# Attention scores as three passes over split operands, the convolved x turned to tokens through DRAM, and branch sums and stream resting in DRAM

## The chip, the cores and the metric

The kernel is one program on 1 core of one Trainium2 chip. A core has a matrix engine (TensorE, PE in the profile), a vector engine (VectorE, DVE), an activation engine (ScalarE, ACT), a general engine (GpSimd, POOL) and a sequencer that issues DMAs (SyncE, SP). Each engine runs its own list of instructions in order, and semaphores make one wait for another. The metric is the device time of one execution in microseconds.

## The reference

Two blocks over 256 tokens of width 2048, all in float32. The first block runs a state-space branch and a gated linear attention branch side by side, merges them, and adds an MLP; the second block is two layers of attention with a gated output. What the change touches:

```python
xbc = silu(causal_depthwise_conv(xbc, conv_w, conv_b))       # 4096 columns of x, 1024 of B, 1024 of C
xs, Bm, Cm = split(xbc)
dt = softplus(dt_raw + dt_bias)
y = ssd_chunked(xs, dt, A, Bm, Cm) + D * xs                  # 64 heads of 64, 8 groups, chunks of 128 tokens
y = grouped_rms_norm(y * silu(z), norm_w, 8)
branch_ssd = y @ w_ssd_branch                                # 4096 -> 2048
merged = sigmoid(gate_ssd) * branch_ssd + sigmoid(gate_gla) * branch_gla
x = layer_norm(ALPHA * x + merged @ w_out)
x = layer_norm(ALPHA * x + squared_relu(x @ w_up) @ w_down)
# then two layers:
scores = q @ k.T * scale ; p = softmax(scores) ; o = p @ v   # three kinds of heads, 4 + 8 heads of 128
x = x + rms_norm((o * silu(gate)) @ w_out2) * norm_post
```

Every product is to be good to float32.

## The kernel before

**Products.** A weight matrix is read from DRAM as half units of 512 KB (`stage`, L128, tiles `ws`, five buffers), and each is split into a rounded high part `wh` (a cast on ACT, L136) and a rest `wl` (a subtraction on DVE, L137); both rings have five buffers. The activations are kept as such a pair too. One product of a 128-row tile is then three passes (`mm3`, L141 to L143: high by high, high by low, low by high) in the format float32r, each 128 x 128 stationary by up to 512 moving columns. The text calls one such pass of 512 columns a pass; a half unit has 12 of them.

**What sets the order.** `drive` walks through all half units in the order of the program. After each product its post-processing is started as a generator (`posts`), and after every second half unit (24 passes) each running generator is stepped once (`tick`). A `yield` in a post-processing therefore moves what follows it behind 24 more passes. The list so made is then ordered, engine by engine, by a scheduler that simulates time and moves an instruction back when it thinks its operands late; at run time each engine keeps that order.

**The state-space stage** (0 to about 650 us). For each of eight groups g there is a product for x and one for z of 96 passes each. `x_post` (L597) takes the x product: `conv_silu` turns it to channels through DRAM (`turn` and `regroup`: VectorE transposes 32 x 32 squares into `sq`, ACT issues four DMAs into the DRAM tile `turn`, SP loads it back as `tn`), convolves it, and leaves it in `xc` with channels on the partitions. Then TensorE turns `xc` back to tokens (L614, two blocks of four transposes), DVE scales that into `xdt`, `xw` and `y`, ACT makes the decay `E` from rows loaded by SP (L601, L624, L626), DVE multiplies it by `cbm` (L627), and TensorE makes `st`, two blocks of `y` and `yo`. `z_post` multiplies by the gate, norms, and turns the result through DRAM into `yT`, the operand of `ssd_branch` (two groups to an operand q; 48 passes for each of four columns n). The sums of the four q rest in four tiles `acc` of the pool `t4` (sixteen buffers of 4 KB a partition) from the first q until the merge.

**The attention layers** (about 2040 to 2857 us). `attend` (L1099) makes the scores of two heads at a time with plain float32 matmuls of 256 moving columns (L1112), the softmax on DVE and ACT, and the product by v. Its operands come from `to_T`, `to_T_t` and `up_T`, which copy the transposed q and k once. The stream `x` rests in four `t4` tiles through a layer and is updated at its end.

Of the kernel before, what the change touches and what calls it, by code (L numbers as in the profile page):

```python
# [17 lines left out]
P = 128  # L18
ST_BUFS, W_BUFS, T_BUFS, S_BUFS = 5, 5, 16, 6
D = 2048  # L20
T = 256
# [57 lines left out]
def tile_blocks(ctx, tc, a, out):  # L79
# [496 lines left out]
    def c_post(i, bh):  # L576
        def post(ps):
            CT = t4([P, 4, T], s="CT")
            yield from conv_silu(ps, 40 + 4 * i, CT)
            while not bh[0].done:  # L580
                yield
            for m in range(2):
                ps = aux([P, 4, P], "cb")
                for g in range(4):
                    nc.tensor.matmul(ps[:, g, :], BT[i][:, g, m * P:m * P + P], CT[:, g, m * P:m * P + P],
                                     start=True, stop=True)
                V.tensor_tensor(cbm[m][:, 4 * i:4 * i + 4, :], ps, U.unsqueeze(1).to_broadcast([P, 4, P]),
                                op=ALU.mult)
            S.copy(CT1[:, 4 * i:4 * i + 4, :], CT[:, :, P:T])
        return post  # L590
# [6 lines left out]
    def x_post(g, need):  # L597
        def post(ps):
            es = [t4([P, 8, P], s="E") for _ in range(2)]
            for m in range(2):  # L600
                nc.sync.dma_start(es[m], acs_rows[g, m].partition_broadcast(P))  # L601
            xc = t4([P, 4, T], s="xc")
            yield from conv_silu(ps, 4 * g, xc)
            for h in need:
                while not h[0].done:
                    yield
            hs = slice(8 * g, 8 * g + 8)
            y = ys[g] = t4([P, 2, 512], s="y")
            xdt = t4([P, 2, 512], s="xdt")
            xw = small([P, 512], "xw")  # L610
            for m in range(2):
                pt = aux([P, 512], "tr")
                for f in range(4):
                    nc.tensor.transpose(pt[:, f * P:f * P + P], xc[:, f, m * P:m * P + P], ident)  # L614
                V.tensor_tensor(heads8(xdt[:, m, :]), heads8(pt),
                                dt[:, m, hs].unsqueeze(2).to_broadcast([P, 8, 64]), op=ALU.mult)
                if m == 0:
                    V.tensor_tensor(heads8(xw), heads8(pt),
                                    dtw[:, hs].unsqueeze(2).to_broadcast([P, 8, 64]), op=ALU.mult)
                V.tensor_tensor(heads8(y[:, m, :]), heads8(pt),  # L620
                                Dbc[:, hs].unsqueeze(2).to_broadcast([P, 8, 64]), op=ALU.mult)
# [25 lines left out]
            V.tensor_tensor(y[:, 1, :], y[:, 1, :], yo, op=ALU.add)  # L647
        return post
# [26 lines left out]

    def ssd_branch(q, n, need):
        def post(ps):
            if q == 0:
                acc[n] = t4([P, 2, 512], s="acc")
            for m in range(2):  # L680
# [12 lines left out]
        return product(lambda: yop[q], [a["w_ssd"][8 * n + 2 * q + s] for s in range(2)], post, need)  # L693
# [216 lines left out]
    def merge(n):  # L910
# [12 lines left out]
        return product(lambda: og[0], [a["w_gla"][4 * n + s] for s in range(4)], post, need=ghs)  # L923
# [174 lines left out]
    def attend(o, pairs, vals, scale, bias=None):  # L1098
# [65 lines left out]

    def to_T(d, src, nft):

        for f in range(0, nft, 2):
            pt = aux([P, 2, T], "tr")
            transpose4(pt, src, f)
            S.copy(d[:, f:f + 2, :], pt)  # L1170

    def layer(l, x, hop, first, nxt):
# [10 lines left out]
        def pre():  # L1183
# [55 lines left out]
        def ckv_post(ps):  # L1239
# [9 lines left out]
            kpT = v["kpT"] = lay([P, 2, T], "kpT")  # L1249
            G.memset(kpT, 0.0)  # L1250
# [3 lines left out]
            for i in range(2):  # L1254
                S.copy(kpT[64 * i:64 * i + 64, i, :], pt[64 * i:64 * i + 64, :])
# [4 lines left out]
        def up_T(ws, op, s):  # L1260

            nk = 2 * len(ws)
            d = t4([P, 4, T], s=s)
            for f in (0, 2):
# [6 lines left out]
                S.copy(d[:, f:f + 2, :], pt)  # L1271
# [21 lines left out]
        def uqr_post(ps):  # L1293
            yield
            d = v["qpT"] = t4([P, 2, T], s="qpT")
# [31 lines left out]
        def akv_post(ps):  # L1327
# [6 lines left out]
            v["kaT"] = t4([P, 2, T], s="kaT")  # L1334
# [9 lines left out]
        def b_post_(ps):  # L1344
# [4 lines left out]
            def pairs(h, m):  # L1349
                ts = slice(m * P, m * P + P)  # L1350
                return [(v["qnT"][:, h, ts], v["knT"][:, h, :]), (v["qpT"][:, h // 2, ts], v["kpT"][:, h % 2, :])]
# [6 lines left out]
        def aq_post(i):  # L1358
            def post(ps):
# [3 lines left out]
                qaT = t4([P, 4, T], s="qaT")  # L1363
                yield from to_T_t(qaT, qa)
# [3 lines left out]
                yield from attend(o, lambda h, m: [(qaT[:, h, m * P:m * P + P], v["kaT"][:, i, :])],  # L1368
# [6 lines left out]
        def c_post_(i):  # L1375
            def post(ps):
# [4 lines left out]
                if i < 2:  # L1381
                    d = v["c", i] = t4([P, 4, T], s="cT")
                    yield from to_T_t(d, c)
# [6 lines left out]
                yield from attend(o, lambda h, m: [(v["c", 0][:, h, m * P:m * P + P], v["c", 1][:, h, :])],  # L1390
# [33 lines left out]
        def y_mid(n):  # L1424
            gb = []

            def pre():
# [4 lines left out]
                yg[n] = t4([P, 2, 512], s="yy")  # L1432

# [75 lines left out]

def _bias(rpb):  # L1510
# [13 lines left out]
def _layout(x):  # L1524
# [5 lines left out]
    cw = a["ssd_conv_w"][0]  # L1530
    o["vec"] = np.ascontiguousarray(np.concatenate(
        [_vec(cw[j]) for j in range(4)]
        + [_vec(a["ssd_conv_b"][0]), _vec(a["ssd_norm_w"][0]), _vec(a["gla_norm_w"][0]),
# [5 lines left out]
    o["w_in"] = np.concatenate([_blocks(w[:, c:c + NB]) for c in W_IN_COLS])  # L1539
# [39 lines left out]
```

## Time and profile before

| | |
|---|---|
| median of 3 runs | 2860.01 us (2857.66 to 2864.86) |
| profiled execution | 2858.03 us, its span 2856.3 us |
| PE busy | 2826.3 us, 99% |
| DVE, ACT busy | 1830.5 us (64%), 1423.6 us (50%) |
| moved by DMA | 617.82 MB, 216 GB/s |
| mean granted clock | 0.997 |

The matmuls are pipelined: the profile gives 0.39 us for one pass of 512 columns, though the next one starts 0.23 us after it. So the cost of a pass is read from the distance of two starts, and not from the length of one. A plain float32 matmul of 128 rows and 256 columns shows up as two records. An engine's idle time is only worth what it holds up: here that is TensorE.

### The profile page before, as it was taken

The page shows a single profiled execution, that of the slowest core. Times are in us where ns is not written, and L with a number is a line of the kernel's source. Part 1 is how long each engine was busy: PE and PEld are TensorE (multiplying, and loading weights), DVE is VectorE, ACT ScalarE, POOL GpSimd, SP SyncE. Part 2 cuts the span into 40 slices and gives each one's busy share as a digit, 9 for nine tenths or more (in the row PEclk, how much of TensorE's full clock was granted, in tenths as well). Part 3 has the DMA queues.
Part 4 walks back from the last instruction along what each step waited for, and adds up shares of the span by engine and source line. Part 5 has one row for each costly group of instructions (what it writes and reads, how often), then busy time and mean ns, then how long its engine had stood idle before and what let it go on. Part 6 is the DMA issues. An engine that isn't in the chain of part 4 may idle for free.

```text
span 2856.3 us, 35047 instructions
## 1 busy us (share of the span) xinstructions
PE 2826.3 (99%) x12928; PEld 2337.8 (82%) x12928; DVE 1830.5 (64%) x2393; ACT 1423.6 (50%) x2013; POOL 36.4 (1%) x49
## 2 busy tenths in 40 slices
PE   9999999999999999999999999999999999999998
PEld 7888888888887878887888888888788888798887
DVE  6877677775844846556665555566776556676564
ACT  5565655554444544445344443344565544655543
POOL 0000000000000000000000000000000000000000
PEclk9999999999999999999999999999999999999999
DMA  8666666666665666674666666667467776567774
GB/s 287 221 226 219 221 221 221 220 221 215 186 198 169 213 200 213 218 269 161 229 227 222 221 212 221 207 222 252 147 217 236 234 238 219 164 214 242 249 234 142
DMA packets 209839, 617.82 MB, mean 216 GB/s; under 512 B 23665, under 2 KB 65009, under 8 KB 209666
## 3 DMA queue, kind: packets, MB, share of 16 engines
q1 hardware_dynamic: 163874, 573.62, 61.2%
q10 hardware_dynamic: 45792, 41.96, 4.7%
q8 instruction: 101, 1.65, 0.2%
q14 instruction: 72, 0.59, 0.1%
HBM read 571.90 MB, written 43.58 MB: 215 GB/s over the span
## 4 chain that ended last, share of the span: by engine, by line
PE 83%; DMA 7%; DVE 4%; ACT 3%; issue 1%; ACTq 1%; SPq 0%; DVEq 0%; POOLq 0%
PE mm L141 26%; PE mm L143 26%; PE mm L142 26%; DMA turn<-sq 3%; DMA tn<-turn 2%; DVE wl L137 2%; DMA ws<-in_w_in 1%; ACT wh L136 1%; PE sc L1112 1%; PE y L637 1%; ACTq L338 1%; DMA E<-acs_rows 1%; PE po L1144 1%; DVE sq L328 0%; PE up L143 0%
## 5 line engine op out<-in xcount | busy, mean ns | idle before, releaser
L137 DVE TENSOR_TENSOR wl<-ws,wh 128x1024 fp32r<-128x1024 f32 (+2 forms) x974 | 1167.9, 1210 | 750.0 <-ACT wh L136 739.8
L136 ACT CAST wh<-ws 128x1024 fp32r<-128x1024 f32 (+2 forms) x974 | 1005.3, 1044 | 979.4 <-PE mm L143 798.0
L141 PE MATMUL mm<-wh,xh 128*128 128x512 f32 x1280 | 503.9, 395 | 0.6 <-ACT wh L136 0.6
L142 PE MATMUL mm<-wl,xh 128*128 128x512 f32 x1280 | 499.8, 391 | 1.1 <-DVE wl L137 1.1
L143 PE MATMUL mm<-wh,xl 128*128 128x512 f32 x1280 | 499.2, 390 | 0.0
L141 PE MATMUL mm<-wh,lnh 128*128 128x512 f32 (+1 forms) x896 | 345.2, 389 | 5.9 <-ACT lnh L304 5.9
L142 PE MATMUL mm<-wl,lnh 128*128 128x512 f32 (+1 forms) x896 | 347.2, 387 | 0.0
L143 PE MATMUL mm<-wh,lnl 128*128 128x512 f32 (+1 forms) x896 | 346.5, 387 | 0.0
L141 PEld LDWEIGHTS mm<-wh,xh 128*128 128x128 f32 x1280 | 240.8, 188 | 55.5 <-issue 3.6
L142 PEld LDWEIGHTS mm<-wl,xh 128*128 128x128 f32 x1280 | 241.0, 188 | 53.6 <-DVE wl L137 2.5
L143 PEld LDWEIGHTS mm<-wh,xl 128*128 128x128 f32 x1280 | 240.9, 188 | 50.4
L141 PEld LDWEIGHTS mm<-wh,lnh 128*128 128x128 f32 x896 | 168.4, 188 | 40.2 <-ACT lnh L304 6.9
L143 PE MATMUL mm<-wh,hT 128*128 128x512 f32 x512 | 199.2, 389 | 0.0
L141 PE MATMUL mm<-wh,hT 128*128 128x512 f32 x512 | 199.2, 389 | 0.0
L142 PE MATMUL mm<-wl,hT 128*128 128x512 f32 x512 | 199.2, 389 | 0.0
L143 PEld LDWEIGHTS mm<-wh,lnl 128*128 128x128 f32 x896 | 168.5, 188 | 34.3 <-DVE lnl L305 0.9
L142 PEld LDWEIGHTS mm<-wl,lnh 128*128 128x128 f32 x896 | 168.5, 188 | 33.4 <-DVE wl L137 0.2
L141 PE MATMUL mm<-wh,hh 128*128 128x512 f32 (+1 forms) x384 | 148.2, 387 | 3.5 <-ACT hh L304 3.5
L142 PE MATMUL mm<-wl,hh 128*128 128x512 f32 (+1 forms) x384 | 148.0, 385 | 0.6 <-DVE wl L137 0.6
L143 PE MATMUL mm<-wh,hl 128*128 128x512 f32 (+1 forms) x384 | 147.1, 384 | 0.0
L141 PEld LDWEIGHTS mm<-wh,hT 128*128 128x128 f32 x512 | 96.1, 188 | 20.0
L143 PEld LDWEIGHTS mm<-wh,hT 128*128 128x128 f32 x512 | 96.1, 188 | 19.9
(366 smaller groups left out, 3403.3 us busy)
## 6 DMA issues: line engine op xcount, KB each, us to landing
ws<-in_w_in SPq DMA_DIRECT2D x494, 512.0 KB
ws<-in_w_up SPq DMA_DIRECT2D x128, 512.0 KB
ws<-in_w_down SPq DMA_DIRECT2D x128, 512.0 KB
ws<-in_w_out SPq DMA_DIRECT2D x96, 512.0 KB
turn<-sq ACTq DMA_DIRECT2D x316, 128.0 KB
tn<-turn SPq DMA_DIRECT2D x79, 512.0 KB
ws<-in_w_ssd SPq DMA_DIRECT2D x64, 512.0 KB
ws<-in_w_gla SPq DMA_DIRECT2D x32, 512.0 KB
```

Of the source, the lines that this page charges most:

```text
L136: S.copy(hi[:, c], st[:, c])
L137: V.tensor_tensor(lo[:, c], st[:, c], f32(hi[:, c]), op=ALU.subtract)
L141: nc.tensor.matmul(ps, l[0], r[0], start=first, stop=False)
L142: nc.tensor.matmul(ps, l[0], r[1], start=False, stop=False)
L143: nc.tensor.matmul(ps, l[1], r[0], start=False, stop=last)
L338: S.dma_start(dv[q], sv[32 * q:32 * q + 32, :].rearrange("j (b r) -> j b r", b=4))
L637: nc.tensor.matmul(py[:, h * 64:h * 64 + 64], es[m][:, h, :], xdt[:, m, h * 64:h * 64 + 64], start=True, stop=True)
L1112: nc.tensor.matmul(ps[:, m, :], l, rr, start=n == 0, stop=n == len(lr) - 1)
L1144: nc.tensor.matmul(po[:, m, :], pT[:, 2 * i + k, m * P:m * P + P], vals(h, k), start=k == 0, stop=k == 1)
```

## The change

- **Scores.** Every operand of a score is kept as a pair of float32r tiles, a rounded copy (ACT) and the rest (a new subtraction on DVE), and each score is made by `mm3`, three passes of 256 columns, in place of one float32 matmul. `kpT` is cleared by a memset of a scratch tile and two casts.
- **Convolved x.** `x_post` no longer uses TensorE: DVE transposes squares of `xc`, `regroup` takes them through DRAM (four DMAs on ACT, one load on SP), and the three scalings read the loaded tile. The columns of x are permuted in the weights for that (`_quarters`). The loads of `E` are issued behind this round trip, where before they were issued at the start of `x_post`.
- **Branch sums.** After each `ssd_branch` the sum goes to DRAM (a DMA on ACT) and is loaded back before the next one and before the merge.
- **Stream.** At the start of each attention layer `x` goes to DRAM, and each quarter is loaded back for its output product.
- **Steps.** `c_post` and both uses of `to_T_t` in the attention get one more `yield`.

```diff
-    def to_T_t(d, src):
+    def to_T_t(d, src, parts=None):
...
-            S.copy(d[:, :, m * P:m * P + P].rearrange("p c (q i) -> p c q i", q=4), by_token(got[0], m))
+            h, l = ((x[:, :, m * P:m * P + P].rearrange("p c (q i) -> p c q i", q=4) for x in parts) if parts else
+                    (d[:, :, m * P:m * P + P].rearrange("p c (q i) -> p c q i", q=4), None))
+            S.copy(h, by_token(got[0], m))
+            if parts:
+                V.tensor_tensor(l, by_token(got[0], m), f32(h), op=ALU.subtract)
...
             yield from conv_silu(ps, 40 + 4 * i, CT)
+            yield
             while not bh[0].done:
...
     def x_post(g, need):
         def post(ps):
-            es = [t4([P, 8, P], s="E") for _ in range(2)]
-            for m in range(2):
-                nc.sync.dma_start(es[m], acs_rows[g, m].partition_broadcast(P))
             xc = t4([P, 4, T], s="xc")
             yield from conv_silu(ps, 4 * g, xc)
             for h in need:
                 while not h[0].done:
                     yield
             hs = slice(8 * g, 8 * g + 8)
+
+            sq = t4([P, 4, 2, 4, 32], s="sq")
+            for m in range(2):
+                V.transpose(sq[:, :, m].rearrange("p a f j -> p f a j"),
+                            xc[:, :, m * P:m * P + P].rearrange("p f (a i) -> p f a i", a=4))
+            got = []
+            yield from regroup(sq, got)
+            xt = got[0].rearrange("p b m f j -> p b m (f j)")
+            es = [t4([P, 8, P], s="E") for _ in range(2)]
+            for m in range(2):
+                nc.sync.dma_start(es[m], acs_rows[g, m].partition_broadcast(P))
...
-            for m in range(2):
-                pt = aux([P, 512], "tr")
-                for f in range(4):
-                    nc.tensor.transpose(pt[:, f * P:f * P + P], xc[:, f, m * P:m * P + P], ident)
-                V.tensor_tensor(heads8(xdt[:, m, :]), heads8(pt),
-                                dt[:, m, hs].unsqueeze(2).to_broadcast([P, 8, 64]), op=ALU.mult)
+            for m in range(2):
+                by_head(xdt[:, m, :], m, dt[:, m, hs])
                 if m == 0:
...
+                    by_head(xw, m, dtw[:, hs])
+                by_head(y[:, m, :], m, Dbc[:, hs])
...
+    acc_rest = [dram.tile([P, 1024], F32, tag=f"acc{n}", name=f"acc{n}") for n in range(4)]
+
+    def acc_load(n):
+        acc[n] = t4([P, 2, 512], s="acc")
+        nc.sync.dma_start(acc[n].rearrange("p m n -> p (m n)"), acc_rest[n])
...
+        def pre():
+            if q:
+                acc_load(n)
+
...
+            S.dma_start(acc_rest[n], acc[n].rearrange("p m n -> p (m n)"))
...
                     for n, (l, rr) in enumerate(lr):
-                        nc.tensor.matmul(ps[:, m, :], l, rr, start=n == 0, stop=n == len(lr) - 1)
+                        mm3(ps[:, m, :], l, rr, n == 0, n == len(lr) - 1)
...
-            S.copy(d[:, f:f + 2, :], pt)
+            S.copy(d[0][:, f:f + 2, :], pt)
+            V.tensor_tensor(d[1][:, f:f + 2, :], pt, f32(d[0][:, f:f + 2, :]), op=ALU.subtract)
+
+
+    x_rest = [dram.tile([P, 1024], F32, tag=f"xs{n}", name=f"xs{n}") for n in range(4)]
...
                     sumsq(x[n][:, m, :], parts[m][:, n:n + 1])
+                nc.sync.dma_start(x_rest[n], x[n].rearrange("p m n -> p (m n)"))
...
-                qaT = t4([P, 4, T], s="qaT")
-                yield from to_T_t(qaT, qa)
+                qaT = two(4, "qaT")
+                yield from to_T_t(None, qa, qaT)
+                yield
...
                 yg[n] = t4([P, 2, 512], s="yy")
+                x[n] = t4([P, 2, 512], s="xs")
+                nc.sync.dma_start(x[n].rearrange("p m n -> p (m n)"), x_rest[n])
```

Three places show where the order of the instructions moved. The first is TensorE in the state-space stage, at group 1: `y` and `yo` are its last products (`E` and `st` its operands), `mm_2107` before and `mm_2070` in the change are the z product of group 2, behind which the first `ssd_branch` product follows. Before:

```order
L142 MATMUL mm_1870<-wl_1941,xh_81 128x512
L143 MATMUL mm_1870<-wh_1940,xl_82 128x512
L637 MATMUL y_2061<-xdt_1902,E_1649 128x64 x8
L643 MATMUL yo_2071<-st_2013,CT_43_109 128x512
L141 MATMUL mm_2107<-wh_1975,xh_81 128x512
L142 MATMUL mm_2107<-wl_1976,xh_81 128x512
```

In the change:

```order
L141 MATMUL mm_2070<-wh_2084,xh_81 128x512
L142 MATMUL mm_2070<-wl_2085,xh_81 128x512
L143 MATMUL mm_2070<-wh_2084,xl_82 128x512
L651 MATMUL y_2106<-xdt_1992,E_1987 128x64 x8
L651 MATMUL y_2154<-xdt_1992,E_1988 128x64 x8
L657 MATMUL yo_2164<-st_2104,CT_43_109 128x512
L141 MATMUL mm_2070<-wh_2084,xh_81 128x512
```

Before, `yo` stands ahead of the first of the 96 passes of that z product; in the change 63 of them are past. The first passes that read the `yT` half of group 1 are the 25th of the `ssd_branch` product in both, so 120 passes lie between before, and 57 in the change.

The second is SP, where the two loads of `E` for group 1 stand (`ws` are weight half units, `tn` a tile loaded back from DRAM). Before:

```order
L128 DMA ws_1426<-in_w_in 128x1024
L128 DMA ws_1446<-in_w_in 128x1024
L601 DMA E_1648<-acs_rows 128x1024
L601 DMA E_1649<-acs_rows 128x1024
L128 DMA ws_1485<-in_w_in 128x1024
```

In the change:

```order
L128 DMA ws_1955<-in_w_in 128x1024
L341 DMA tn_1949<-turn_1908 128x1024
L128 DMA ws_1973<-in_w_in 128x1024
L620 DMA E_1987<-acs_rows 128x1024
L620 DMA E_1988<-acs_rows 128x1024
L128 DMA ws_2011<-in_w_in 128x1024
```

The loads moved behind `tn_1949`, the load that ends the new round trip of `xc`, and with it behind the wait of that load for its DRAM writes.

The third is ACT in the first attention layer, at the second block of four `a` heads: `turn` is the DRAM write of the turned q, `qaT` (`qaTh`) the copy that the scores wait for. Before:

```order
L338 DMA turn_17335<-sq_17332 32x4x256 x4
L136 CAST wh_17515<-ws_17362 128x1024
L1147 ACTIVATE ao_17157<-po_17381,rec_17168 128x128 x2
L1147 ACTIVATE ao_17157<-po_17388,rec_17179 128x128 x2
L136 CAST wh_17535<-ws_17401 128x1024
L1138 COPY pT_17433<-tn_17376 128x4x128 x2
L136 CAST wh_17593<-ws_17419 128x1024
L374 COPY qaT_17331<-tn_17395 128x4x128 x2
```

In the change:

```order
L338 DMA turn_17497<-sq_17494 32x4x256 x4
L136 CAST wh_17699<-ws_17526 128x1024
L136 CAST wh_17717<-ws_17567 128x1024
L1164 COPY pT_17542<-tn_17492 128x4x128 x2
L136 CAST wh_17776<-ws_17585 128x1024
L136 CAST wh_17794<-ws_17623 128x1024
L1173 ACTIVATE ao_17302<-po_17545,rec_17317 128x128 x2
L376 CAST qaTh_17446<-tn_17502 128x4x128 x2
```

Four casts of weights stand between the write and the copy where there were three. On TensorE the scores moved further: the cast ahead of the write is released by a pass that is 51 passes ahead of these scores before, and 84 in the change.

## Rows read from the trace of the kernel before

**Rows 1.** The page, parts 1 and 4: busy time; chain by line.

```profile
PE 2826.3 (99%) x12928; PEld 2337.8 (82%) x12928; DVE 1830.5 (64%) x2393; ACT 1423.6 (50%) x2013; POOL 36.4 (1%) x49
...
PE mm L141 26%; PE mm L143 26%; PE mm L142 26%; DMA turn<-sq 3%; DMA tn<-turn 2%; DVE wl L137 2%; DMA ws<-in_w_in 1%; ACT wh L136 1%; PE sc L1112 1%; PE y L637 1%; ACTq L338 1%; DMA E<-acs_rows 1%; PE po L1144 1%; DVE sq L328 0%; PE up L143
```

**Rows 2.** Two stretches: each engine's busy us (count), clock, DMA.

```profile
140.00:660.00 520.00, 518.32 (x2414) 427.71 (x2413) 378.75 (x529) 303.06 (x474) 5.58 (x8) 1.00 0.68 222
1400.00:1600.00 200.00, 200.00 (x884) 165.65 (x883) 116.37 (x117) 82.16 (x86) 0.00 (x0) 1.00 0.68 223
```

**Rows 3.** Timeline of PE: passes of a plain product.

```profile
1000.08 0.39 PE L141 MATMUL mm<-wh,xh 128*128 128x512 f32 x1
...
1008.70 0.39 PE L143 MATMUL mm<-wh,xl 128*128 128x512 f32 x1
```

**Rows 4.** Timeline of PE: one block of four transposes at line 614.

```profile
158.79 0.39 PE L143 MATMUL mm<-wh,xl 128*128 128x512 f32 x1
159.03 0.60 PE L614 MATMUL tr<-cst,xc 128*128 128x128 f32 x4
...
159.93 0.40 PE L143 MATMUL mm<-wh,xl 128*128 128x512 f32 x1
```

**Rows 5.** Instructions of lines 1112 and 614, whole span.

```profile
0.00:2857.00 2857.00, 38.75 (x160) 30.96 (x160) 1.00 0.66 216
0.00:2857.00 2857.00, 9.75 (x64) 8.03 (x64) 1.00 0.66 216
```

**Rows 6.** Timeline of PE: first and last score of one block.

```profile
2132.67 0.59 PE L1112 MATMUL sc<-knT,qnT 128*128 128x256 f32 x2
...
2139.15 0.59 PE L1112 MATMUL sc<-kpT,qpT 128*128 128x256 f32 x2
```

**Rows 7.** Timeline of PE: split passes of 256 columns.

```profile
2125.80 0.28 PE L143 MATMUL up<-kvh,wl 128*128 128x256 f32 x1
...
2126.52 0.29 PE L143 MATMUL up<-kvh,wl 128*128 128x256 f32 x1
```

**Rows 8.** Waits of PE, by what ended them.

```profile
PE sc L1112 <- ACT qaT L374: 4.4, 2, 3.3
...
PE cb L585 <- DVE CT L557: 1.2, 2, 0.8
```

**Rows 9.** Timeline of PE: scores behind a wait of 3.26 us.

```profile
2218.77 3.66 PE L1112 MATMUL sc<-kaT,qaT 128*128 128x256 f32 x8 [3.26 <-ACT qaT L374]
2221.86 0.82 PE L141 MATMUL mm<-wh,lnh 128*128 128x512 f32 x1
```

**Rows 10.** Granted clock (behind POOL's column) after that wait.

```profile
2220.00:2224.00 4.00, 4.00 (x14) 3.13 (x13) 2.58 (x5) 2.86 (x11) 0.00 (x0) 0.71 0.41 122
```

**Rows 11.** Timeline: group 1 from yo to its yT's reader.

```profile
231.31 1.13 PE L643 MATMUL yo<-st,CT 128*128 128x512 f32 x2 [0.57 <-ACT st L633]
243.88 2.04 ACTq L338 DMA_DIRECT2D turn<-sq  x4
251.37 0.33 SPq L341 DMA_DIRECT2D tn<-turn  x1
257.74 1.13 DVE L366 SCALAR_TENSOR_TENSOR yT<-tn,vec,yT 128x128 fp32r<-128x128 f32 x4
259.52 0.39 PE L141 MATMUL mm<-wh,yT 128*128 128x512 f32 x1
```

**Rows 12.** Timeline of ACT: eight instructions on one tile E.

```profile
224.10 2.46 ACT L624 ACTIVATE E<-E,acs 128x128 f32<-128x128 f32 x8 [4.84 <-DMA E<-acs_rows]
```

**Rows 13.** Chain in order of time: two transfers, issue to landing.

```profile
185.62 4.32 DMA turn<-sq
...
216.24 7.83 DMA E<-acs_rows
```

**Rows 14.** Groups by line: DVE on E.

```profile
L627 DVE TENSOR_TENSOR E<-E,cbm 128x1024 f32<-128x1024 f32 x16 | 19.5, 1218 | 5.8 <-ACT E L626 5.8
```

**Rows 15.** The page, part 2: all DMA traffic.

```profile
DMA packets 209839, 617.82 MB, mean 216 GB/s; under 512 B 23665, under 2 KB 65009, under 8 KB 209666
```

More of the change, by code (lines that the diff above doesn't have):

```diff
@@ L692, in post @@
             yield
-        return product(lambda: yop[q], [a["w_ssd"][8 * n + 2 * q + s] for s in range(2)], post, need)
+        return product(lambda: yop[q], [a["w_ssd"][8 * n + 2 * q + s] for s in range(2)], post, need, pre=pre)
     def gate_tanh(col, row, n):
@@ L922, in post @@
                 yield from to_op(mg, 4, *mop[0], 4 * n, mul=0.5)
-        return product(lambda: og[0], [a["w_gla"][4 * n + s] for s in range(4)], post, need=ghs)
+        return product(lambda: og[0], [a["w_gla"][4 * n + s] for s in range(4)], post, need=ghs,
+                       pre=lambda: acc_load(n))
     gate_tanh(GG0, 1, 0)
@@ L1163, in attend, with two, part @@
         yield
+    def two(nft, s):
+        if nft == 2:
+            d = t4([P, 2, 2, T], F32R, s=s)
+            return d[:, 0], d[:, 1]
+        return t4([P, nft, T], F32R, s=s + "h"), t4([P, nft, T], F32R, s=s + "l")
+    def part(ap, *i):
+        return tuple(x[i] for x in ap)
     def to_T(d, src, nft):
@@ L1248, in ckv_post @@
             yield from to_op(ckv, 2, *v["ckv"], 0, scale=vec[:, V_KVN + 2 * l:V_KVN + 2 * l + 2])
-            kpT = v["kpT"] = lay([P, 2, T], "kpT")
-            G.memset(kpT, 0.0)
+            kpT = v["kpT"] = tuple(lpool[0].tile([P, 2, T], F32R, tag=f"kpT{i}", name=nm("kpT")) for i in range(2))
+            zero = small([P, 512], "zero")
+            G.memset(zero, 0.0)
+            for i in range(2):
+                V.tensor_copy(kpT[i], zero.rearrange("p (i t) -> p i t", i=2))
             pt = aux([P, T], "tr")
@@ L1254, in ckv_post @@
             for i in range(2):
-                S.copy(kpT[64 * i:64 * i + 64, i, :], pt[64 * i:64 * i + 64, :])
+                hs = slice(64 * i, 64 * i + 64)
+                S.copy(kpT[0][hs, i, :], pt[hs, :])
+                V.tensor_tensor(kpT[1][hs, i, :], pt[hs, :], f32(kpT[0][hs, i, :]), op=ALU.subtract)
         cqj = product(hopf, w2(0), cq_post, need=first, pair=(0,))
@@ L1262, in up_T @@
             nk = 2 * len(ws)
-            d = t4([P, 4, T], s=s)
+            d = two(4, s)
             for f in (0, 2):
@@ L1270, in up_T @@
                             (op[0][:, k, :], op[1][:, k, :]), k == 0, k == nk - 1)
-                S.copy(d[:, f:f + 2, :], pt)
+                S.copy(d[0][:, f:f + 2, :], pt)
+                V.tensor_tensor(d[1][:, f:f + 2, :], pt, f32(d[0][:, f:f + 2, :]), op=ALU.subtract)
             return d
@@ L1294, in uqr_post @@
             yield
-            d = v["qpT"] = t4([P, 2, T], s="qpT")
+            d = v["qpT"] = two(2, "qpT")
             to_T(d, v["qp"], 2)
@@ L1333, in akv_post @@
             yield
-            v["kaT"] = t4([P, 2, T], s="kaT")
+            v["kaT"] = two(2, "kaT")
             to_T(v["kaT"], ka, 2)
@@ L1350, in pairs @@
                 ts = slice(m * P, m * P + P)
-                return [(v["qnT"][:, h, ts], v["knT"][:, h, :]), (v["qpT"][:, h // 2, ts], v["kpT"][:, h % 2, :])]
+                al = slice(None)
+                return [(part(v["qnT"], al, h, ts), part(v["knT"], al, h)),
+                        (part(v["qpT"], al, h // 2, ts), part(v["kpT"], al, h % 2))]
             yield from attend(o, pairs, lambda h, k: v["vb"][:, k, h * P:h * P + P], 192.0 ** -0.5)
@@ L1367, in post @@
                 o = v["o", i] = t4([P, 2, 512], s="ao")
-                yield from attend(o, lambda h, m: [(qaT[:, h, m * P:m * P + P], v["kaT"][:, i, :])],
+                yield from attend(o, lambda h, m: [(part(qaT, slice(None), h, slice(m * P, m * P + P)), part(v["kaT"], slice(None), i))],
                                   lambda h, k: v["va"][:, k, i * P:i * P + P], 128.0 ** -0.5)
@@ L1381, in post @@
                 if i < 2:
-                    d = v["c", i] = t4([P, 4, T], s="cT")
-                    yield from to_T_t(d, c)
+                    d = v["c", i] = two(4, "cT")
+                    yield from to_T_t(None, c, d)
                     yield
@@ L1389, in post @@
                 o = v["o", 3] = t4([P, 2, 512], s="ao")
-                yield from attend(o, lambda h, m: [(v["c", 0][:, h, m * P:m * P + P], v["c", 1][:, h, :])],
+                yield from attend(o, lambda h, m: [(part(v["c", 0], slice(None), h, slice(m * P, m * P + P)), part(v["c", 1], slice(None), h))],
                                   lambda h, k: v["c", 2][:, k, h * P:h * P + P], 128.0 ** -0.5, a["c_bias"][l])
@@ L1507, in _vec, with _quarters @@
     return np.asarray(v).reshape(-1, P).T
+def _quarters(w):
+    return w.reshape(w.shape[0], -1, 4, 4, 32).transpose(0, 1, 3, 2, 4).reshape(w.shape)
 def _bias(rpb):
@@ L1529, in _layout @@
     o["consts"] = _consts()
-    cw = a["ssd_conv_w"][0]
+    cw, cb = (np.concatenate([_quarters(v[:, :4096]), v[:, 4096:]], axis=1)
+              for v in (a["ssd_conv_w"][0], a["ssd_conv_b"]))
     o["vec"] = np.ascontiguousarray(np.concatenate(
         [_vec(cw[j]) for j in range(4)]
-        + [_vec(a["ssd_conv_b"][0]), _vec(a["ssd_norm_w"][0]), _vec(a["gla_norm_w"][0]),
+        + [_vec(cb[0]), _vec(a["ssd_norm_w"][0]), _vec(a["gla_norm_w"][0]),
            _vec(a["ln1_g"][0]), _vec(a["ln1_b"][0]),
@@ L1538, in _layout @@
     w = a["w_in"][0]
-    o["w_in"] = np.concatenate([_blocks(w[:, c:c + NB]) for c in W_IN_COLS])
+    o["w_in"] = np.concatenate([_blocks(_quarters(w[:, c:c + NB]) if XBC0 <= c < XBC0 + 4096 else w[:, c:c + NB])
+                                for c in W_IN_COLS])
     o["w_dtlr"] = _blocks(np.concatenate([w[:, LR0:LR0 + 16], w[:, DT0:DT0 + 64]], axis=1), 16, 80)[0]
```

9 lines of the change are left out of this document (5 added, 4 removed).

## The prediction

> **What bounds the kernel now.** The page's busy times come first, and the chain by line beside them: TensorE is busy 99% of the span, and three quarters of the chain that ended last are the three passes of a product [rows 1]. Then the table of stretches, for the state-space stage and, as a comparison, for a stretch of plain products at the full clock: in the first TensorE is busy 518.3 of 520 us, while DVE works 379 and ACT 303 [rows 2]. So DVE and ACT have 27% and 42% of that stage free, and work added there costs only what it makes late. The unit of the sum is a pass: 38 passes in 8.62 us, 0.2268 us each [rows 3]. An edit thus counts in two ways: work taken off TensorE, and an operand that comes later than the passes between its producer and its reader give it time for.
>
> The sum is made on the profiled execution (2858.03 us, its span 2856.3). The median of the runs is 2.0 us higher, and the forecast is stated against that median. About 0.3%, or 8.6 us, is what a measurement of this kernel can tell from no change.
>
> **Transposes of x, removed.** A block of four stands between starts 158.79 and 159.93; of these 1.14 us three passes are 0.68, so four transposes cost 0.46 [rows 4]. There are 64 of them [rows 5], 16 blocks: -7.4 us.
>
> **Scores.** 160 records are 80 matmuls [rows 5]. From the first to the last of a block of 16 are 15 steps in 6.48 us, 0.432 each [rows 6], 34.6 us in all. A float32r pass with the same 256 columns costs 0.120 (six steps in 0.72) [rows 7]; 240 of them are 28.8 us. So -5.8 us.
>
> [...]
>
> **Waits that go.** The scores of the a heads wait 4.4 us for `qaT`, in two places, 3.3 in the longer [rows 8]. [...] Together 3.26 + 1.4 + 1.1 in the other layer, some 6 us. By the order of TensorE the cast ahead of the q write is released 84 passes before these scores instead of 51: 33 passes, 7.5 us, more than the 3.3 it was late, though one more cast and a subtraction stand in the path. So -6 us, bounds 0 (the wait stays) and -6. What comes late next would be the low half, one subtraction behind the copy. The wait of `cb` for `CT`, 1.2 us [rows 8], goes with the extra step of 24 passes: -1.2.
>
> The gains are 7.4 + 5.8 + 6.0 + 1.2 = 20.4 us.
>
> **A wait that comes: the first `ssd_branch`.** Its passes read the `yT` of group 1. Before, `yo` of group 1 starts at 231.31, and the first reader of the `yT` half that ends last starts at 259.52, when that half has been done since 258.87 (257.74 + 1.13): 0.65 us to spare [rows 11]. What lies between is gate, norm, squares, four writes on ACT at 243.88, the load on SP at 251.37 and the four operations of DVE, 27.6 us in all. In the change `y` and `yo` stand 63 passes later, because the operand comes by a round trip first, and the reader has not moved: 57 passes for 120. 63 x 0.2268 = 14.3 us less, minus the 0.65 to spare: 13.6 us of idle TensorE. If the second `y` also waits for `E`, up to 2 us more. If TensorE stands still the casts run ahead, and ACT and DVE serve the chain sooner: 12.6 us of it lie between `yo` and the write, with casts and squares among them, of which 1 to 8 may go. I take 13, bounds 7 and 17. Queued behind the waiting pass are all weights of that product; nobody else needs TensorE's result meanwhile, and what was missed is not made up since every later pass follows in order. After the idle time the clock falls as in rows 10; an idle 3.26 us cost 1.4 there, a longer one I put at 2, bounds 1.4 and 5. So +15. The later q have a whole product more between (168 passes, 38 us, for a chain of 27.6) and do not wait.
>
> The round trip's own length is in the trace: the write took 4.32 us from issue to landing [rows 13], and from the write's issue at 243.88 to the load's at 251.37 are 7.5 us, to the DVE operations behind it some 4 more [rows 11], so about 11.5. [...]
>
> **`E` behind the round trip.** Its load now starts after the trip: turn 4 to 5 us, `tn` 4 to 5, `E` 7.8 [rows 13], two times 2.46 on ACT [rows 12], two exponentials at 1.05 on ACT, and 1.2 on DVE [rows 14]: about 25 us from the turn to the first `y`. By the order `y` stands about that far behind in the groups 0 and 2 to 7, with 1 to 2 us to spare. Such a spare is met in most groups and missed by little in some: I take one miss of 3 us, the spread between the transfers counted above, as the nearer value, with bounds 0 and 24 (3 us in each of 8 groups).
>
> **What is hidden.** DVE gets 16 transposes of squares, about 11 us, in a stage where it has 141 us free; low parts in the attention, some 20 us, where TensorE's share is as high. ACT gets 32 issues for the turns, four of them in 2.04 us [rows 11], and 16 for the sums; SP 40 loads and stores, whose waits stand ahead of weight loads in its list. DMA gets 64 transfers of 512 KB, 33.6 MB, 5% of 617.82 [rows 15]; the stage moves 222 GB/s and its queues are busy 0.68 [rows 2]. Cover is the ring of weights: five `ws` and five `wh` tiles of 12 passes, 27 us of products. As long as a wait on SP or a burst is shorter than that it costs nothing: 0, and if the cover is gone, a bound of +10.
>
> **Sum.** -20.4 + 15 + 3 = -2.4 us: 2855.6 by the profiled execution, about 2857.5 by the median.
>
> **Rivals.** *No long wait* (faster): the chain behind `yo` shrinks because TensorE's stop sets free what it shares ACT and DVE with, and `E` comes in time. -20.4 + 7 + 1.4 = -12, so 2848. For it: ACT's casts stand inside the chain. Against it: the two DMA waits in it, 11.5 us, don't shrink. *`E` late in each group* (slower): the path to `E` is as long as the passes give it time for; with 3 us in each of 8 groups in place of 3 in all, the sum is -20.4 + 15 + 24 = +18.6, so 2878.5. The place is the first `y` of each group; it decides once `E` is later than 2 us beyond my count. For it: before, `E` already took 7.83 us to land and ACT waited 4.84 for it [rows 12, 13]. Against it: E's path is counted with 4 to 5 us for each way, which is what loaded queues show. *The stream of weights suffers* (slower): SP's waits for its round trips hold up weight loads, or 5% more traffic in bursts empties the ring; the bound of +10 on top of the sum gives +7.6, 2867.5, and with the waits' clock some 2871. Against it: 27 us of cover. *The score wait stays* (no change): the extra step is eaten by the extra casts, -2.4 + 6 = +3.6, so 2863.5.
>
> **Chances.** The forecast's case 0.45 (0.38 within 0.3%, 0.04 below, 0.03 above), no long wait 0.29, `E` late 0.16, stream of weights 0.05 (counted as slower), score wait stays 0.05 (no change). Faster 0.33, no change 0.43, slower 0.24. The forecast's own range is 2849 to 2866; to hold 8 in 10 it reaches to 2843, past the centre of the first rival, and to 2874, into the lower half of the second; signs of both kinds hold over half.
>
> **What would show it.** No transposes behind the x products, and score passes 0.12 us apart. TensorE idle some 13 us at the first pass that reads group 1's `yT`, released by DVE or ACT on `yT`, with a granted clock well below 1 just behind; none at the later q. `y` waiting for DVE's product on `E`: a few us in all by the forecast, 24 by the rival. No wait of `sc` for `qaT`. More than 222 GB/s in the state-space stage with TensorE's share there, apart from the two waits, still at 99%. The forecast is wrong if the long wait is under 7 or over 17 us, if `E` costs over 8, or if a wait for `wh` or `ws` shows.

## The result, and the profile after

The changed kernel takes 2874.68 us (median of 9 runs, 2867.94 to 2878.75) against 2860.01 us before: a ratio of 1.0051, with a 95% interval of 1.0041 to 1.0061. It is 0.5% slower, where no change was forecast, and 0.7 us above the upper end of the range. The profiled execution is the shortest of the nine, 2867.94 us, so the trace shows 9.9 of the 14.7 us; what the other executions lose beyond that, no trace of this kernel shows. Two executions count in no time or ratio below: one of 4046.18 us at a granted clock of 0.653, and one of 16386.11 us at 1.000.

The page of the kernel after, parts 1 and 2, answers to [rows 1, 15]:

```profile
PE 2818.1 (98%) x12944; PEld 2331.0 (81%) x12944; DVE 1861.3 (65%) x2445; ACT 1425.5 (50%) x2013; POOL 38.1 (1%) x49
...
DMA packets 222511, 651.38 MB, mean 227 GB/s; under 512 B 25073, under 2 KB 70513, under 8 KB 222338
```

TensorE works 8 us less than before, and the span is 9.5 us longer: 17.7 us more of idle time. The stretches (columns as in [rows 2]: the busy time of PE, PEld, DVE, ACT and POOL, the granted clock, the DMA's share and GB/s) say where, and at what clock; the second is the 4 us behind the longest wait:

```profile
140.00:660.00 520.00, 495.53 (x2231) 405.00 (x2230) 369.87 (x518) 288.55 (x460) 4.90 (x7) 0.98 0.74 245
270.00:274.00 4.00, 3.84 (x9) 3.10 (x10) 3.85 (x11) 2.79 (x7) 0.00 (x0) 0.50 0.65 237
```

In the state-space stage TensorE idles 24.5 us where it idled 1.7. Its last pass there starts at 683.9 us for 662.0 before: the stage loses 21.9 us. Behind it 12.3 come back, 11.5 of them from 2019 us (before) on, which is the attention and the little ahead of it, so that the last product ends 9.6 us later. The waits of TensorE over the whole span (us in total, times, longest):

```profile
PE mm L142 <- DVE wl L137: 12.7, 8, 4.1
PE mm L141 <- ACT yT L363: 7.7, 1, 7.7
PE mm L141 <- ACT lnh L304: 4.5, 2, 2.2
PE mm L141 <- ACT hh L304: 3.6, 2, 2.5
PE st L645 <- DVE xw L626: 3.2, 1, 3.2
PE y L651 <- DVE E L641: 2.7, 4, 1.1
```

The waits for `qaT` and `CT` of [rows 8] are gone, as forecast. The wait for `yT` is there. But the largest group, the wait for `wl`, the low half of a weight, was priced at nothing. The waits of DVE, and of ACT, between 140 and 700 us say what the halves are late for; the third line is ACT's in the kernel before, where DVE had no such wait:

```profile
DVE xdt L626 <- DMA tn<-turn: 45.3, 8, 7.3
```

```profile
ACT E L638 <- DMA E<-acs_rows: 50.7, 8, 7.7
```

```profile
ACT E L624 <- DMA E<-acs_rows: 16.0, 7, 5.7
```

Once per group DVE stands at the first scaling of x until the tile `tn` is back from DRAM, and ACT stands at the first operation on `E`. The timeline of group 3 shows what stands behind them (start, length, engine; in brackets the idle time before):

```profile
344.84 1.79 ACTq L338 DMA_DIRECT2D turn<-sq  x4
347.83 2.36 DVE L137 TENSOR_TENSOR wl<-ws,wh 128x1024 fp32r<-128x1024 f32 x2 [0.78 <-ACT wh L136]
349.60 1.06 ACT L136 CAST wh<-ws 128x1024 fp32r<-128x1024 f32 x1
351.47 0.33 SPq L341 DMA_DIRECT2D tn<-turn  x1
351.58 1.05 ACT L136 CAST wh<-ws 128x1024 fp32r<-128x1024 f32 x1 [0.91 <-PE mm L143]
352.35 1.03 SPq L620 DMA_DIRECT2D E<-acs_rows  x2
357.49 0.69 DVE L626 TENSOR_TENSOR xdt<-tn,dt 128x512 f32<-128x512 f32 x1 [7.30 <-DMA tn<-turn]
359.06 0.39 PE L141 MATMUL mm<-wh,xh 128*128 128x512 f32 x1
360.24 2.45 ACT L638 ACTIVATE E<-E,acs 128x128 f32<-128x128 f32 x8 [7.62 <-DMA E<-acs_rows]
360.51 2.35 DVE L137 TENSOR_TENSOR wl<-ws,wh 128x1024 fp32r<-128x1024 f32 x2
361.78 0.50 PE L142 MATMUL mm<-wl,xh 128*128 128x512 f32 x1 [2.33 <-DVE wl L137]
362.60 1.03 ACT L136 CAST wh<-ws 128x1024 fp32r<-128x1024 f32 x1
363.31 0.63 PE L141 MATMUL mm<-wh,xh 128*128 128x512 f32 x1
```

The last subtraction ends at 350.19, the next begins at 360.51: for 10.3 us DVE stands for `tn` (7.3) and then works off five scalings, while the subtractions of the two half units cast at 349.60 and 351.58 wait in its list. ACT stands too: its next cast, at 362.60, is behind the first operations on `E`. From 350.19 on TensorE has passes until 359.3, that is for 9.1 us; then it waits 2.33, until the first of the two subtractions is done. In the last row it goes on at half speed: passes 0.43 us apart, at a granted clock of 0.50 from 362.88 to 365.87.

### The profile page after: what moved, and what is told of

Same layout as the page of the kernel before. It is cut to its first block, busy times and chain, and to the rows that moved or that the text cites. A ratio compares the mean times of both kernels' runs of the same rounds, so it can differ in the third digit from the quotient of the medians.

```text
span 2865.8 us, 35292 instructions
## 1 busy us (share of the span) xinstructions
PE 2818.1 (98%) x12944; PEld 2331.0 (81%) x12944; DVE 1861.3 (65%) x2445; ACT 1425.5 (50%) x2013; POOL 38.1 (1%) x49
## 2 busy tenths in 40 slices
DMA packets 222511, 651.38 MB, mean 227 GB/s; under 512 B 25073, under 2 KB 70513, under 8 KB 222338
## 4 chain that ended last, share of the span: by engine, by line
PE 86%; DMA 5%; DVE 4%; ACT 2%; issue 1%; ACTq 1%; SPq 0%; POOL 0%; DVEq 0%; POOLq 0%
PE mm L141 27%; PE mm L142 27%; PE mm L143 27%; DMA turn<-sq 2%; DVE wl L137 1%; DMA E<-acs_rows 1%; DMA tn<-turn 1%; PE po L1170 1%; ACT wh L136 1%; ACT E L638 1%; DVE xc L558 1%; DMA ws<-in_w_in 1%; ACTq L338 1%; PE y L651 1%; PE sc L141 0%
## 5 line engine op out<-in xcount | busy, mean ns | idle before, releaser
L142 PE MATMUL mm<-wl,xh 128*128 128x512 f32 x1280 | 501.7, 392 | 10.3 <-DVE wl L137 10.3
L142 PEld LDWEIGHTS mm<-wl,hT 128*128 128x128 f32 x512 | 96.1, 188 | 20.0
L141 PEld LDWEIGHTS mm<-wh,hT 128*128 128x128 f32 x512 | 96.1, 188 | 19.9
```

What stands on the lines that cost most here:

```text
L141: nc.tensor.matmul(ps, l[0], r[0], start=first, stop=False)
L142: nc.tensor.matmul(ps, l[0], r[1], start=False, stop=False)
```

## Experiments

The theory that was tested: late operands at the head of an engine's list hold up the weight splits queued behind them (DVE for `tn`, ACT for `E`), and together with the first `ssd_branch` they cost what the stage lost. The rival: the added traffic and the resting of the branch sums cost it. Medians are of 4 to 11 runs; ratios are to runs of the kernel before in the same set, with their 95% intervals, and where two kernels are compared below, it is by their ratios.

**One part at a time.** `x_post` and the weights of x as before, all else as changed:

```diff
-            yield from regroup(sq, got)
...
+                for f in range(4):
+                    nc.tensor.transpose(pt[:, f * P:f * P + P], xc[:, f, m * P:m * P + P], ident)
```

> The changed kernel with x_post and the weights of x as before (transposes on TensorE, E loaded early); scores in three passes, branch sums and stream in DRAM stay. Theory 1 (the new round trip of x puts waits at the head of the lists of DVE, 45 us in 8 waits for tn, and of ACT, 51 us in 8 waits for E, and the weight splits queued behind them empty the ring): the state-space stage is as before, TensorE waits for wl there fall from 12.7 us to under 3, the wait for yT is gone, and the attention keeps its gain of about 12 us: 2848. Rival (the traffic of the resting branch sums, with the store's issue on ACT, is what the stage loses by): the losses on wl stay, 2860 or more.

2852.38 us, 0.9961 (0.9947 to 0.9975): 4 us over the number expected, which is a ratio of 0.9958 and within the interval. The round trip of x, with the loads of `E` behind it, turns a gain into a loss. TensorE's waits for `wl` between 140 and 700 us are 3.0 us here. Then the scores alone:

```diff
-                        nc.tensor.matmul(ps[:, m, :], l, rr, start=n == 0, stop=n == len(lr) - 1)
+                        mm3(ps[:, m, :], l, rr, n == 0, n == len(lr) - 1)
```

> The kernel before with the scores in three passes alone (with the two extra steps in the attention; x, branch sums, stream and CT as before). By both theories the attention gains 5.8 us by the passes and up to 6 by the wait for qaT, and the low parts cost nothing: 2848 to 2849, ratio 0.996. If resting the sums and the stream costs or gives something of its own, this differs from the kernel with x as before by it; theory 1 expects under 3 us between the two, the rival 10 or more.

2848.87 us, 0.9952 (0.9940 to 0.9964), as expected; faster than both kernels, and the fastest of those that leave nothing out. The two intervals overlap: resting sums and stream cost nothing that can be measured. One caution comes with this kernel's trace: its state-space stage is that of the kernel before, and yet its passes end there 4.5 us later than in the trace before. So a few us in the stage, between two single traces, are not yet a difference between two kernels.

**Where `E` is loaded, and one step more.**

```diff
+            es = [t4([P, 8, P], s="E") for _ in range(2)]
+            for m in range(2):
+                nc.sync.dma_start(es[m], acs_rows[g, m].partition_broadcast(P))
             xc = t4([P, 4, T], s="xc")
...
             xt = got[0].rearrange("p b m f j -> p b m (f j)")
-            es = [t4([P, 8, P], s="E") for _ in range(2)]
-            for m in range(2):
-                nc.sync.dma_start(es[m], acs_rows[g, m].partition_broadcast(P))
```

> The changed kernel with E loaded at the start of x_post again. ACT's wait for E (51 us in 8) goes, DVE's wait for tn (45 us in 8) stays, and y of group 1 stands 39 passes earlier. Theory 1a (DVE's wait at the head of its list is what empties the ring): the waits for wl stay at 8 us or more, only the wait for yT shrinks by some 5 us: 2868 to 2870. Theory 1b (ACT's wait for E holds the casts): the waits for wl go, and with the smaller wait for yT it comes to 2858 to 2862.

2870.16 us, 1.0025 (1.0016 to 1.0034), just above theory 1a: the wait for `yT` falls from 7.7 to 1.1 us, and the waits for `wl` over the whole span are still 7.4 (theory 1a: 8 or more). DVE's wait for `tn`, which was to stay, fell to 21.1 us, and ACT's for `E` only to 20.6. New are 9.2 us in which the `ssd_branch` product waits until DVE has read the sums of the z product (`sz`). So this run alone does not tell the two theories apart.

```diff
+            yield
             y = ys[g] = t4([P, 2, 512], s="y")
```

> The changed kernel with one more step (24 passes) between the loads of tn and E and the work that reads them. DVE's wait for tn and ACT's for E both fall from 45 and 51 us to under 15. Theory 1: TensorE's waits for wl in the state-space stage fall to under 4 us, and each group's y waits no more; the wait for yT of group 1 grows by 2 to 5 us since yo stands 9 passes later: in all 2862 to 2868. Rival (traffic of the sums, or the store on ACT): the waits for wl stay, and with the longer wait for yT the time is 2876 to 2880.

2874.32 us, 1.0045 (1.0032 to 1.0057): between the two ranges, for a reason that divides. From group 3 on the stage was clean but for one wait of 3.1 us: four of five stretches of 288 passes ran 0.85 to 0.94 us shorter than before, which is what two blocks of transposes cost. But groups 1 and 2 lost 27.7 us. There, with the later `yo`, the first products of `ssd_branch` wait twice (6.7 for `sz`, 4.9 for `yT`), and 4.9 for a `wl` and 3.2 for `acc` come beside them; what the rest is made of was not followed up. DVE's and ACT's own waits fell only to 32.0 and 45.7 us, against my expectation.

**The first branch later.**

```diff
         h = product(xop, w_in(XBC0 + 512 * g), x_post(g, ch + [dth]), need=[dth])
+        if g == 3:
+            for n in range(2):
+                ssd_branch(0, n, zh[0:2])
```

> The changed kernel with the first two products of ssd_branch (q = 0) put behind the x product of group 3, 96 passes later. Theory: the wait for yT (7.7 us and half speed behind it for some 2) goes entirely, the waits on wl further on stay, since the heads of DVE's and ACT's lists still wait for tn and E: 2864 to 2867. Rival (the delay of group 1 is one chain, and what is not lost at the first branch is lost at the next operand, so that nothing is won): 2872 to 2876.

2871.94 us, 1.0035 (1.0023 to 1.0048). The wait for `yT` is gone, and by the ratios only 4.6 us with it, with intervals that overlap: `st` waits 6.5 us for DVE's scaling `xw` (3.2 in the change), and `wl` 12.9. It lies at the rival's lower end. All three together, and the same with `E` left behind the trip:

> The changed kernel with all three: E loaded at the start of x_post, one more step between the load of tn and its readers, the first two products of ssd_branch 96 passes later. By the theory that three waits (DVE for tn, ACT for E, the first branch) took what the transposes gave, all are gone and the state-space stage ends some 5 to 7 us ahead of the kernel before: 2842 to 2848, under the kernel with the scores alone (2848.9). Rival (traffic, the store's issue and SP's list hold up the weights whatever the order): 2855 or more.

> As the kernel with all three, but E is loaded behind tn as in the change; one more step and the first branch later. It tells E's late load from the rest: ACT's wait for E stays (45.7 us in 8 waits with the step alone). If casts held behind E do empty the ring, the waits on wl and the time lie above the kernel with all three by 5 us or more; if DVE's wait for tn was the one that counted, the two are within 2 us.

2895.70 us, 1.0122 (1.0106 to 1.0138), and 2866.53 us, 1.0024 (1.0014 to 1.0034). The first missed by 50 us in the wrong direction. The two waits that were to go did not: DVE still stands 35.1 us for `tn` and ACT 25.4 for `E`. Between 140 and 700 us ACT also waits for weights, 3.5 us in one place in the change, and TensorE most of all for DVE to read the z product's sums:

```profile
ACT wh L136 <- DMA ws<-in_w_in: 26.9, 10, 6.3
```

```profile
PE mm L141 <- DVE sz L402: 13.1, 3, 4.5
PE st L646 <- DVE xw L627: 7.8, 3, 3.8
PE mm L142 <- DVE wl L137: 6.4, 3, 4.5
```

ACT's wait for weights does not explain the loss by itself: it is 28.2 us in the faster kernel without both waits (below). Two `E` tiles held a step longer out of the sixteen of `t4`, with SP waiting for a free tile ahead of weight loads, is a reading, not tested. Why this kernel is so slow stays open, and the two kernels don't price `E`.

**The store on SP.**

```diff
-            S.dma_start(acc_rest[n], acc[n].rearrange("p m n -> p (m n)"))
+            nc.sync.dma_start(acc_rest[n], acc[n].rearrange("p m n -> p (m n)"))
```

> The changed kernel with the stores of the branch sums issued by SP in place of ACT. The store's issue stood 3.2 us on ACT in the longest case, with casts behind it, 10 us before TensorE's longest wait on wl (4.1 us, group 6). If that is what makes this wait, it goes with its clock: 2867 to 2870. If the wait comes from DVE standing for tn, it stays: 2872 to 2876; SP's list, with the store's wait ahead of weight loads, may make it worse.

2873.82 us, 1.0045 (1.0031 to 1.0058), the change's time: the issue on ACT is not what the time is lost by. The wait of 4.1 us itself is not in this trace, but `y` waits 9.4 us for `E`, in five places, where it waited 2.7 in the change's.

**The waits taken away, the work kept.** The scalings read `xc` and nobody reads `tn`; or `E` is made from `cbm` and nobody reads the rows; or both. Every transfer is still made (651.38 MB in all three). In the second and third kernel the decay goes into two further tiles of `t4`, and without a wait some instructions also stand a little elsewhere in the lists (in the third `yo` of group 1 comes 15 passes earlier than in the change).

```diff
-            xt = got[0].rearrange("p b m f j -> p b m (f j)")
+            xt = xc.rearrange("p b (m j) -> p b m j", m=2)
```

```diff
-                    S.activation(e[:, h, :], e[:, h, :], AF.Relu, scale=-1.0,
+                    S.activation(e[:, h, :], cbm[m][:, h, :], AF.Relu, scale=-1.0,
```

> The changed kernel in which the three scalings read xc as it lies in place of the tile tn loaded back (x is not turned: its values reach the wrong places; the round trip is still made, and nobody reads it). The instructions and the traffic are those of the change, DVE has no wait for tn at the head of its list (45 us in 8 before). If that wait emptied the ring, the waits on wl in the state-space stage fall from 11 to under 3 us and the time to 2858 to 2864; ACT's wait for E (51 us) stays. If it was ACT's wait for E, or the traffic, wl stays near 11 us: 2868 to 2872.

> The counterpart: the scalings read tn as in the change, and the decay E is made from cbm and not from the rows loaded for it (its values are wrong; the rows are loaded and not read). ACT has no wait for E (51 us in 8), DVE still waits for tn. If ACT's wait, with casts queued behind it, emptied the ring, the waits on wl fall to under 3 us: 2860 to 2865. If it was DVE's, they stay near 11, and only the waits of y for E (2.7 us) and a part of the first branch go: 2866 to 2871.

> Both at once (x not turned, E not from its rows): all instructions and transfers of the change, and neither wait. If waits are what the state-space stage lost by, it keeps the gain of the transposes: 2842 to 2848, with under 5 us of idle TensorE there. If the traffic of the round trips and of the resting sums, or the added work of DVE and ACT, took it, the time stays above 2858.

Without the wait for `tn` 2879.47 us, 1.0071 (1.0058 to 1.0083); without that for `E` 2868.65, 1.0033 (1.0020 to 1.0045); without both 2851.72, 0.9971 (0.9961 to 0.9981). The stretch from 140 to 700 us, the first number behind the comma being TensorE's busy time: the change, without `tn`'s wait, without `E`'s, without both:

```profile
140.00:700.00 560.00, 535.22 (x2417) 437.42 (x2416) 399.20 (x556) 313.99 (x499) 5.60 (x8) 0.98 0.75 245
```

```profile
140.00:700.00 560.00, 534.86 (x2371) 438.71 (x2370) 391.64 (x543) 309.20 (x492) 5.58 (x8) 0.97 0.73 242
```

```profile
140.00:700.00 560.00, 534.69 (x2402) 436.85 (x2401) 396.76 (x555) 315.37 (x499) 5.58 (x8) 0.98 0.73 247
```

```profile
140.00:700.00 560.00, 547.79 (x2498) 450.99 (x2497) 410.47 (x568) 325.32 (x509) 5.59 (x8) 0.99 0.74 255
```

TensorE idles 24.8, 25.1, 25.3 and 12.2 us. One wait taken away gives little: by the ratios the time goes up by 5.7 us without `tn`'s wait and down by 5.1 without `E`'s, both with intervals that overlap the change's, and other waits come in its place. With the wait for `tn` gone, ACT still stands 45.0 us for `E`, and TensorE's `y` waits for it; with that for `E` gone, DVE still stands 47.8 us for `tn`. TensorE's waits in that stretch, first without `tn`'s wait, then without `E`'s, then without both:

```profile
PE y L651 <- DVE E L641: 13.0, 5, 3.7
PE mm L141 <- ACT wh L136: 4.7, 2, 4.3
PE mm L141 <- ACT yT L363: 4.5, 1, 4.5
PE mm L142 <- DVE wl L137: 2.9, 5, 1.0
```

```profile
PE mm L142 <- DVE wl L137: 13.9, 6, 4.9
PE st L645 <- DVE xw L626: 6.3, 2, 3.5
PE mm L141 <- ACT yT L363: 5.0, 1, 5.0
```

```profile
PE mm L141 <- ACT yT L363: 9.5, 1, 9.5
PE mm L142 <- DVE wl L137: 2.0, 2, 1.0
```

Both expectations that one of the two would be the cause fell; that traffic and added work are not, stands: without the waits they ran beside TensorE at 255 GB/s, and every stretch of 288 passes from group 3 on was 0.96 to 0.99 us shorter than before. The change's ratio less this one is 0.0080: the two waits together, with what the lists change by when they go, cost 23 us.

**Mixed.** Groups 0 to 2 with transposes, 3 to 7 with the trip and the step:

```diff
-        h = product(xop, w_in(XBC0 + 512 * g), x_post(g, ch + [dth]), need=[dth])
+        h = product(xop, w_in(XBC0 + 512 * g), (x_post if g < 3 else x_post_d)(g, ch + [dth]), need=[dth])
```

> Groups 0 to 2 with x as before (transposes, E early), groups 3 to 7 with the round trip and one more step between its load and the readers; scores, sums and stream as in the change. With the step alone the groups 3 to 7 each came out 0.92 us shorter than before, and groups 0 to 2 lost all. So 5 x 0.92 = 4.6 us under the kernel with x as before (2852.4): 2846 to 2849. If the loss was not one of the first groups but of the number of groups that take the round trip, it lies at 2858 or more.

2852.44 us, 0.9971 (0.9961 to 0.9982). Against the step in every group (1.0045) the loss is gone with the first groups, but the 4.6 us don't appear in the median: against transposes everywhere (0.9961) it is a tie. The trace says where they stay: groups 3 to 7 take 2.1 us longer than before, and TensorE waits some 4.5 us there (`wl`, `wh`, `y` and `sz`), with ACT still standing 33.6 us for `E` and DVE 23.7 for `tn`.

**The first branch, and the sums, priced alone.** On the kernel without both waits: the first branch 96 passes later (edit as above), and the sums left in their tiles (`acc_load` and the store taken out):

> As the kernel with both unread (x not turned, E not from its rows), and the first two products of ssd_branch 96 passes later. With no other wait left in the stage this prices the first branch: if its 9.5 us of idle TensorE and the half speed behind it are a loss of their own, some 11 us go and the time is 2839 to 2843. If the delay of group 1 is only handed on (as it seemed in the changed kernel, where moving the branch alone gave under 3 us), it stays at 2848 or more.

> As the kernel with both unread (x not turned, E not from its rows), and the branch sums stay in their tiles, as before the change. It prices the stores and loads of the sums (16 each of 512 KB) where no other wait hides them. Theory: they cost nothing, within 2 us of the kernel with both unread (2851.7). Rival (they take DMA time and places in the lists): 2846 or less; or, if four tiles fewer in the pool are missed, over 2855.

2844.81 us, 0.9945 (0.9930 to 0.9959): the first branch is worth 7 us, between the two numbers expected, though 7.0 us of short waits for `wl` came in seven other places. And 2849.81 us, 0.9962 (0.9949 to 0.9974): the sums' 2.6 us can't be told from nothing.

## Why the prediction was wrong

**What held.** Transposes: -7.4 forecast, and each clean group ran shorter by about 0.92 for its two blocks. Scores: passes still 0.12 us apart in the trace after (the first at 2160.59, the 48th at 2166.18, 47 steps), so 48 take 5.7 us for the 6.9 of 16 float32 matmuls; five blocks give 6. With the wait for `qaT` gone the trace of the change gains 11.5 us from 2019 us on and that of the scores alone 13.7, for 11.8 forecast; over all fifteen traces with these scores it is 9 to 14.

The rows' 5.8 us for the scores stands: three passes at 0.12 us are 0.36, against 0.432 for one float32 matmul [rows 6], and so they save 17%. Of the 6 us for the wait for `qaT`, the 1.4 are the four scores' 3.09 us [rows 9] less four times the 0.432; no run shows that term alone, only the gain from 2019 us on.

**What was mis-sized.** The first `ssd_branch`: 13 us and 2 of clock forecast; 7.7 and 1.9 measured. The chain was indeed shorter than counted, but not in the place given. The timeline after:

```profile
248.46 1.08 PE L657 MATMUL yo<-st,CT 128*128 128x512 f32 x2
260.66 0.80 ACTq L338 DMA_DIRECT2D turn<-sq  x2
265.65 0.33 SPq L341 DMA_DIRECT2D tn<-turn  x1
269.60 1.71 ACT L363 ACTIVATE yT<-tn,vec 128x256 fp32r<-128x256 f32 x4 [3.20 <-DMA tn<-turn]
270.16 0.80 PE L141 MATMUL mm<-wh,yT 128*128 128x512 f32 x1 [7.70 <-ACT yT L363]
```

From `yo` to the write are 12.2 us, as before (12.6, [rows 11]). TensorE stands only from 262.46 on, behind the write, so its stop can have set nothing free there. From write to load took 5.0 us instead of 7.5, and from load to reader 4.5, where 7.5 us were counted to the end of the half that is made last: the waiting pass reads the high part, which ACT makes first. That the wait came out within its bounds is in part luck.

For the 11.5 us counted from the write's issue to the operations behind the load, the two legs make 9 us here, but in group 3 the same trip of x takes 12.65 (344.84 to 357.49).

**What failed.** The step that failed is the part on what is hidden, with its price of 0 for waits and its cover of 27 us. It looked at SP's waits and at work added to DVE and ACT, and did not name what is queued behind `xdt` on DVE and behind `E` on ACT: the weight splits. The cover was not five `ws` and five `wh` tiles in a row: what counts is the halves already split, and those lasted 9.1 us in group 3 against a stop of 10.3. The +3 for `E` counted only TensorE's wait for it (2.7 measured, 13.0 once `tn` no longer hid it), and not ACT's 51 us. In place of 3 the two waits cost 23. The whole sum can be read from the runs: without both waits and with the branch later the kernel gains 15.7 us (0.9945) where gains of 20.4 were forecast; the first branch takes back 7.4 and the two waits 22.9, which makes 14.6 together by the ratios, for 14.7 measured by the medians. The gains fell short in the stage: in that trace it ends 1.1 us earlier than before, for 8.6 forecast, with 7.0 us of waits for `wl` in it. The prediction's own sign for this, a wait for `wh` or `ws`, named the neighbours of the tile that was late.

In group 3 both engines kept to the order of their lists: on DVE two subtractions whose casts were done by 352.63 ran only at 360.51, behind the scaling that waited until 357.49, and on ACT the next cast ran at 362.60, behind the operations on `E` that began at 360.24 after a wait of 7.62 us. That order is what I didn't weigh against this change.

**The rivals.** That `E` is late in each group (0.16, 2878.5) came near in time and was half of the mechanism; its sign, waits of `y` for `E`, is 2.7 us in the change's trace, 9.4 with the store on SP and 13.0 without `tn`'s wait (2879.47), for 24 forecast. That the weights suffer (0.05) named the right victim, with the wrong cause: DVE's and ACT's lists, not SP's or the traffic.

Open is what the other executions of the changed kernel lose beyond the profiled one. A hint is the trace with the store on SP, taken in an execution of 2876.04 us: its stage is 6.2 us longer than in the change's trace, and the waits of `y` for `E` are the 9.4 us named above.

## What to carry to other kernels

Ahead of a DMA round trip, ask for each engine that reads its result what stands behind the reader in that engine's list, and how many microseconds of finished operands the consumer holds; the stop is that engine's whole wait plus the work it does before it comes back to the stream (in group 3, 7.3 us and 3.0 on DVE). Where two waits come from one late trip, taking one away can show nothing (here 5.7 us up and 5.1 down, against 23 down for both): take both away, with all the work kept, before calling either harmless. And set a saving against the waits that its new path can bring: here 7.4 us of transposes stood against 23.

## What was not expected of the hardware

The price of a wait of TensorE was not its length alone. In the state-space stage of the change, 24 passes in all behind the waits of 7.70, 4.13 and 2.33 us started 0.43 us apart instead of 0.23 (7, 10 and 7 of them, with one or two between the two steps beside them), at a granted clock of 0.50 (270.75 to 273.74, 586.50 to 590.00 and 362.88 to 365.87). That added 1.9, 2.4 and 1.5 us; nothing of the kind followed the wait of 3.19 us that ended at 234.57 (passes 0.23 us apart, clock 1.00 from 235 to 239), nor those of about 1 us (clock 1.00 behind the one of 1.22 at 169.82).
